# One level of Strassen's algorithm for the second layer's query, key and value projections

## The chip, the cores and the metric

The kernel runs on one core of a Trainium2 chip. The metric is the device time of one execution in microseconds (us). The kernel as it stands takes 2287.54 us (median of three runs, 2286.23 to 2288.77).

## The reference

Two encoder layers run over 1024 tokens of width 1024. Each is a token mixer, a residual sum with layer normalization (LN), a gated feed-forward block (FFN), and again a residual sum with LN. The mixer of the first layer (layer A) is latent attention; that of the second (layer B) is differential attention. What the change touches is the first matrix product of layer B:

```
h = x @ w_in                                  # x (1024, 1024), w_in (1024, 3072)
q, k, v = jnp.split(h, [qk_w, 2 * qk_w], axis=-1)
q = q.reshape(b, s, 8, 2, 64)                 # 8 heads, two softmax maps of width 64
k = k.reshape(b, s, 8, 2, 64)
v = v.reshape(b, s, 8, 128)
...
logits = (q_b . k) * scale - slopes * dist    # per map; a chunk mask on top
a = softmax(map 0) - lam * softmax(map 1)
o = a @ v                                     # then RMS norm per head, and w_o
```

## The kernel before

**Precision.** Every product of float32 values is made of three passes through TensorE. An operand is split into a high part (ScalarE casts it to fp32r) and a low part (VectorE or GpSimd subtracts the high part from the value); the passes are high times high, high times low, low times high (`mm3`, L140 to L145, and L545 or L814 for the FFN). A "split" below is this pair of instructions; `op_unit` (L504) splits one 128x512 block.

**Stages.** The program runs layer A's attention (to about 370 us), its output projection, FFN 0 with its up and down products (to 1079 us), layer B's attention with its projections (1079 to 1495 us and a tail), its output projection, and FFN 1. Both FFNs already use one level of Strassen's algorithm; the projections of layer B don't.

**Around the change.** FFN 0's down product ends with a sum over 11 blocks into four PSUM banks (`dw`, L814), which completes token rows 0 to 3 (a row is a block of 128 tokens); rows 4 to 7 were normalized earlier. `to_xT` (L187) transposes the normalized rows by TensorE and splits them into `xT`, the token operand of the projections, which stays in SBUF in high and low parts. `values_b` (L1262) makes the values of two heads for one row: 24 matmuls with 256 moving columns. `proj_b` (L1281) makes a head's queries or keys for half of the tokens: 24 matmuls with 512 columns; it splits the result straight from PSUM into the layout of the scores (two maps of 64 partitions each; a DMA on GpSimd's queue copies the high part of a query to the other 64 partitions). Weights come by `load_w` (L128), 512 KB each: ScalarE casts 128x1024, GpSimd subtracts 128x1024.

**Order.** A framework's scheduler lays out each engine's instruction order when the program is built; engines then run in that order and wait for each other by semaphores. `attention` (L261) walks through 64 blocks (8 heads with 8 rows of queries). Block `b` issues the scores of block `b + 2`, the transposes of its own softmax, and what `fill` holds for slot `b`. For layer B `fill` puts head 0's projections and values in front of slot 0 and those of head `h` into the slots of head `h - 1`:

```
for j, slot in enumerate((2, 3, 5, 6) if h < H - 1 else (1, 2, 3, 5)):
    at(b + slot, proj_b, h, j // 2, j % 2 if h < H - 1 else 1 - j % 2)
```

At slot 54 `begin_out` (L1410) closes the space of `xT`, and the output projection's weights are loaded there (L361). Nearly all loads and stores are issued by SP, whose queue is in order: a transfer that waits holds up all behind it.

Of the kernel before, what the change touches and what calls it, by code (L numbers as in the profile page):

```python
# [9 lines left out]
F32 = mybir.dt.float32  # L10
# [6 lines left out]
P = 128  # L17
S = 1024
# [20 lines left out]
LAST_ORDER = (6, 7, 4, 5, 2, 3, 0, 1)  # L39


@with_exitstack
def trunk(
# [10 lines left out]
    w_b_qk,  # L54
    w_b_v,
# [131 lines left out]
    def to_xT(y, xT, tb, name, where):  # L187
        hf, c = tb // 4, (tb % 4) * P
        for kq in range(0, KD, 4):
            pt = where[kq // 4](f"xTp_{name}_{kq}")  # L190
            for k in range(4):
                tr(pt[:, k * P:(k + 1) * P], y[:, (kq + k) * P:(kq + k + 1) * P])
            pv = pt.rearrange("p (k t) -> p k t", k=4)
            hi = xT[0][hf][:, kq:kq + 4, c:c + P]
            lo = xT[1][hf][:, kq:kq + 4, c:c + P]
            A.copy(hi, pv)
            V.tensor_tensor(lo, pv, f32(hi), ALU.subtract)

    def new_xT(pool, name):
        t = {  # L200
            (p, hf): pool.tile([P, KD, 512], F32R, tag=f"xT{p}{hf}", name=f"xT{p}{hf}_{name}")
            for hf in range(2) for p in range(2)
        }
        return [[t[p, hf] for hf in range(2)] for p in range(2)]


# [74 lines left out]
    def out_proj(side, w_o, o_dram, x_src, x_dst, lng, lnb, xo):  # L281


        with tc.tile_pool(name="op0", bufs=2, side=side, reuse_waits="tile") as pool:
# [21 lines left out]
            for tb in LAST_ORDER:  # L306
# [152 lines left out]
    def raw_x(y, xo, tb, name):  # L459
# [16 lines left out]
        if tb < 4:  # L476
# [5 lines left out]
            V.tensor_tensor(b21, b21, b12, ALU.add)  # L482
# [33 lines left out]
    def ffn(side, xo, xst, pending, layer, x_src, x_dst, lng, lnb, next_x, spare=()):  # L516
# [211 lines left out]
        pool = st.enter_context(tc.tile_pool(name=f"fd{layer}", bufs=1, side=side, reuse_waits="tile"))  # L728
        stx = ExitStack()
# [182 lines left out]
        else:  # L912
# [11 lines left out]
            junk = wp.tile([P, 2, 512], F32, tag="wr", name=f"junk_{nm}", bufs=2)  # L924
# [6 lines left out]
            for t in range(4):  # L931
# [5 lines left out]
                rest.append(lambda t=t, y=y: to_xT(y, new, t, f"{nm}_{t}", (ps_t, ps_s)))  # L937
# [5 lines left out]
    xs_dr = [dr.tile([S, D], F32, name=f"xs_dr{l}") for l in range(3)]  # L943

# [141 lines left out]
    with ast as st:  # L1086
# [88 lines left out]
        def mix_a(h, g):  # L1175
# [3 lines left out]
            A.copy(ob, po[:, :256])  # L1179
# [15 lines left out]
        for h in range(1, H):  # L1195
# [9 lines left out]
            at(b + (7 if h < H - 1 else 5), k_nope, h, 1)  # L1205
        at(12, constants)
# [12 lines left out]
    xst, wts = ExitStack(), {}  # L1219

    def next_x():
        pool = xst.enter_context(tc.tile_pool(name="xp0", bufs=1, side="right", reuse_waits="tile"))
        wts["v", 0] = [load_w(w_b_v[0, kh], 1024, f"wbv0_{kh}") for kh in range(2)]
        return new_xT(pool, "f0")

    xo, stacks = x_pools("m0", "right")
# [9 lines left out]
    xT, rest, normed = ffn(  # L1236
# [6 lines left out]
    with ExitStack() as st:  # L1243
        lp = st.enter_context(tc.tile_pool(name="b1l", bufs=5, reuse_waits="tile"))
        pool = st.enter_context(tc.tile_pool(name="b1", bufs=2, reuse_waits="tile"))
        ptp = st.enter_context(tc.tile_pool(name="b1p", bufs=4, reuse_waits="tile"))
# [3 lines left out]
        qt = [big_tile(f"bq{j}") for j in range(2)]  # L1250
        kt = [big_tile(f"bk{j}") for j in range(2)]
        ob = big_tile("bo", F32)
        q_hi = [qt[0][:, 0], qt[0][:, 1], qt[1][:, 0]]
# [264 lines left out]
```

## Time and profile before

| what | value |
|---|---|
| median of the runs | 2287.54 us |
| span of the profiled execution (from the page; it gives no other time of that execution) | 2284.9 us |
| TensorE (PE) busy | 2244.2 us, 98% of the span |
| VectorE (DVE), ScalarE (ACT), GpSimd (POOL) busy | 68%, 45%, 38% |
| moved by DMA | 288.28 MB, 126 GB/s on average |
| layer B's projections and most of its attention | 1075 to 1495 us of the span |

"Busy" of PE counts overlapping matmuls once; a matmul of 512 columns is listed with about 390 ns, but the next one starts after about 227 ns. So its cost in a chain of matmuls is read from starts, not from durations. PEld is the loading of weights into the array, which overlaps. A line of a group reads: source line, engine, operation, output and inputs with their shapes, count, busy time, mean of one, and the idle time before. In the list of waits, the figures are total us, times and the longest.

### The profile page before, as it was taken

The numbers are of one execution on the slowest core, as the hardware profiler recorded it, in microseconds if no ns is written. First come the engines' busy times: TensorE is split into PE (matmuls) and PEld (weight loads), VectorE is DVE, ScalarE is ACT, GpSimd is POOL, SyncE is SP. The second block draws the span as 40 slices with busy tenths as digits, with TensorE's granted clock in tenths as the row PEclk, the third lists the DMA queues.
The fourth block names the chain that finished last, engine by engine and source line by source line (L and its number), as shares of the span: only waits on it lengthen the run. The fifth ranks groups of instructions, "written<-read, shape, count | busy, mean of one in ns | idle before, by whom it ended". The sixth has DMA issues, their size and how long they took to land.

```text
span 2284.9 us, 31183 instructions
## 1 busy us (share of the span) xinstructions
PE 2244.2 (98%) x11410; PEld 1910.8 (84%) x11410; DVE 1561.1 (68%) x2901; ACT 1017.7 (45%) x2097; POOL 861.2 (38%) x687
## 2 busy tenths in 40 slices
PE   8999999999999999999999999999999999999997
PEld 8899998878888887888888898987778888887886
DVE  5667675687666658777476766676777666658777
ACT  4455574442333324345465655564432233324353
POOL 2223241114444435455432423221014444436564
PEclk9999999999999999999999999999999999999999
DMA  5010125344344428454311202154254132337353
GB/s 202 14 37 29 41 72 201 138 137 154 144 157 173 157 103 333 176 182 145 106 43 33 70 24 70 29 203 150 92 172 155 70 133 75 134 120 307 140 206 122
DMA packets 105546, 288.28 MB, mean 126 GB/s; under 512 B 7969, under 2 KB 30113, under 8 KB 94897
## 3 DMA queue, kind: packets, MB, share of 16 engines
q1 hardware_dynamic: 100976, 275.87, 34.0%
q0 software_dynamic: 4416, 10.42, 1.6%
q8 instruction: 90, 1.47, 0.3%
q14 instruction: 64, 0.52, 0.1%
HBM read 205.00 MB, written 77.07 MB: 123 GB/s over the span
## 4 chain that ended last, share of the span: by engine, by line
PE 87%; DVE 5%; DMA 3%; ACT 2%; issue 1%; POOL 1%; SPq 0%; DVEq 0%; POOLq 0%; ACTq 0%
PE gb L545 14%; PE gc L545 10%; PE ga L545 8%; PE dw L814 7%; PE s_a L219 4%; PE zp_a L413 4%; PE dx L814 3%; PE s_b L219 3%; PE dv L814 3%; PE dy L814 3%; PE bp L143 3%; PE bp L144 3%; PE bp L145 3%; PE o_a L258 2%; PE o_b L258 2%; PE hq L1019 1%
## 5 line engine op out<-in xcount | busy, mean ns | idle before, releaser
L499 ACT CAST op_g<-gr 128x512 fp32r<-128x512 f32 x240 | 146.8, 621 | 370.8 <-PE gb L545 183.5
L500 POOL TENSOR_TENSOR op_g<-gr,op_g 128x512 fp32r<-128x512 f32 x104 | 145.8, 1407 | 247.6 <-ACT op_g L499 139.4
L500 DVE TENSOR_TENSOR op_h<-rh,op_h 128x512 fp32r<-128x512 f32 x154 | 164.5, 1096 | 62.3 <-ACT op_h L499 62.3
L545 PE MATMUL ga<-xh_m,op_g 128*128 128x512 f32 x512 | 168.1, 389 | 0.0
L499 ACT CAST op_h<-rh 128x512 fp32r<-128x512 f32 x154 | 92.9, 619 | 140.3 <-PE dx L814 37.6
L814 PE MATMUL dw<-op_w_t,op_h 128*128 128x512 f32 x660 | 151.4, 390 | 0.0
L814 PEld LDWEIGHTS dw<-op_w_t,op_h 128*128 128x128 f32 x660 | 123.5, 188 | 26.1 <-DVE op_h L500 0.6
L225 ACT ACTIVATE l_b<-l_b,mx_b 128x256 f32<-128x256 f32 (+7 forms) x128 | 99.5, 778 | 79.2 <-DVE mx_b L222 77.4
L1322 POOL TENSOR_SCALAR l_b<-l_b,r_b,cst 128x128 f32<-128x128 f32 (+3 forms) x64 | 52.8, 825 | 204.1 <-DVE r_b L227 193.2
L814 PE MATMUL dx<-op_w_b,op_h 128*128 128x512 f32 x528 | 123.5, 394 | 5.1 <-ACT op_w_b L499 3.9
L500 POOL TENSOR_TENSOR op_w_t<-tt,op_w_t 128x512 fp32r<-128x512 f32 x66 | 98.1, 1490 | 80.3 <-ACT op_w_t L499 80.3
L814 PEld LDWEIGHTS dx<-op_w_b,op_h 128*128 128x128 f32 x528 | 99.7, 190 | 28.6 <-ACT op_w_b L499 4.7
L500 DVE TENSOR_TENSOR op_g<-gr,op_g 128x512 fp32r<-128x512 f32 x136 | 110.7, 817 | 15.7 <-ACT op_g L499 15.4
L545 PE MATMUL gb<-t4h_f,op_g 128*128 128x512 f32 x352 | 115.9, 390 | 3.4 <-DVE tmp L628 3.4
L500 POOL TENSOR_TENSOR op_g<-s,op_g 128x512 fp32r<-128x512 f32 x40 | 55.2, 1379 | 168.7 <-ACT op_g L499 160.4
L545 PE MATMUL gc<-b22h_f,op_g 128*128 128x512 f32 x352 | 115.4, 389 | 0.8 <-ACT op_g L499 0.8
L545 PE MATMUL gb<-t2h_f,op_g 128*128 128x512 f32 x352 | 115.5, 390 | 0.4 <-DVE op_g L500 0.4
L545 PE MATMUL gc<-t1h_f,op_g 128*128 128x512 f32 x352 | 115.6, 390 | 0.2 <-ACT op_g L499 0.2
L545 PE MATMUL gb<-t3h_f,op_g 128*128 128x512 f32 x352 | 115.2, 389 | 0.0
L545 PEld LDWEIGHTS ga<-xh_m,op_g 128*128 128x128 f32 x512 | 96.1, 188 | 19.9
L143 PE MATMUL bp<-xT_f,h_wb 128*128 128x512 f32 x256 | 103.0, 402 | 0.0
L145 PE MATMUL bp<-xT_f,l_wb 128*128 128x512 f32 x256 | 101.6, 397 | 0.0
(382 smaller groups left out, 6732.8 us busy)
## 6 DMA issues: line engine op xcount, KB each, us to landing
gr<-in_w_gu SPq DMA_DIRECT2D x44, 1024.0 KB, 6.9
rh<-h_dr SPq DMA_DIRECT2D x28, 1024.0 KB, 5.4
h_dr<-sh SPq DMA_DIRECT2D x22, 1024.0 KB, 5.0
h_dr<-hp SPq DMA_DIRECT2D x22, 768.0 KB, 4.1
tt<-in_w_dn SPq DMA_DIRECT2D x22, 512.0 KB, 8.7
rh<-h_dr SPq DMA_DIRECT2D x14, 768.0 KB, 4.4
wo_dr<-op_pwo SPq DMA_DIRECT2D x16, 512.0 KB, 3.3
z<-xs_dr SPq DMA_DIRECT2D x16, 512.0 KB, 10.1
```

What stands on the lines that cost most here:

```text
L143: T.matmul(ps_out, lh, rh, start=(i == 0), stop=False)
L144: T.matmul(ps_out, lh, rl, start=False, stop=False)
L145: T.matmul(ps_out, ll, rh, start=False, stop=(i == n - 1))
L219: T.matmul(s[:, :w], lh, rh[:, ks], start=(j == 0), stop=(j == len(q_pass) - 1))
L225: ends["exp"] = A.activation(l[:, :n], l[:, :n], AF.Exp, bias=mx, scale=-1.0, accum_out=sm).ins
L258: T.matmul(po[:, c], a, b[:, j % 2, c], start=st, stop=sp_, skip_group_check=True)
L413: T.matmul(m, a[:, h, :], self.wo[h][w][:, c], start=(start and h == heads[0] and a is oh and w == 0), stop=(stop and h == heads[-1] and a ...
L499: A.copy(hi, src)
L500: return eng.tensor_tensor(lo, src, f32(hi), ALU.subtract).ins
L545: T.matmul(o, w[:, a, kc], x[b][:, k, :], start=(first and k == 0 and (a, b) == (0, 0)), stop=(k == 3 and a == 1), skip_group_check=True,)
L814: T.matmul(o, h[:, a, c], w[:, b_], start=(first and (a, b_) == (0, 0)), stop=(last and a == 1), skip_group_check=True,)
L1322: G.tensor_scalar(l1[:, :n], l1[:, :n], r1, nlam, ALU.mult, ALU.mult)
```

## The change

The products of `x` with 3072 columns are cut into 12 units of 256 columns: 8 of one head's queries and keys (`qk`), 4 of two heads' values (`v`). In each unit one level of Strassen's algorithm (the form with seven products) halves the inner dimension, the 256 columns and the 1024 tokens. A unit then has products "1" to "7", each of 12 matmuls with 512 columns, and sums around them. The operands change as follows.

- **Weights.** Products 1, 2 and 4 use blocks of the matrix itself (256 KB each, `w_b`); 6, 3, 7 and 5 use sums of blocks. These sums are made during layer A's attention: 48 parts are loaded (`take`), summed in four GpSimd instructions of 128x128 (`combine`) and stored to `ws_dr` (`put`). In layer B each of the 84 operands is loaded and split (ACT, POOL), four products ahead.
- **Tokens.** Rows 4 to 7 are transposed while FFN 0's last down sum still runs (`early`), and are the operands of products 1 and 2. Rows 0 to 3 come by `raw_x`, as in the FFNs. The seven token operands are 2 MB each, in high and low parts. There is room for two of them (`xop`); so all seven are stored to `x_dr`, and the units go through five passes of 3, 3, 3, 2 and 1 units. Pass 0 forms its five operands on the chip, passes 1 to 4 load theirs again from `x_dr` (26 loads of 2 MB). An operand's space is loaded again (`ready`) when its last product has been issued.
- **Results.** The joins of the products are DVE instructions on 128x512. Queries and keys are split, stored to `qk_dr` and fetched from there in the layout of the scores (`fetch_qk`). Values come out transposed and are turned by TensorE (`turned`), 64 transposes in all.
- **Order.** 27 of the 84 products stand in front of the attention, 3 at its start, and 54 in slots 0 to 50.

```diff
@@ out_proj of layer A
+                    elif tb == LAST_ORDER[1]:
+                        behind(i, ends["ob"])
@@ ffn, around FFN 0's last down sum
+        if next_x is not None:
+            next_x.begin()
...
             whole(y4, from_h(2, "4", ("o",)), t4(), False)
+            with tc.high_priority(100):
+                for t in range(4, 8):
+                    next_x.early(z[t], t)
+                for i in range(4):
+                    next_x.weights(i)
             stx.close()
-            new = next_x()
-            with tc.high_priority(60):
-                for t in range(4, 8):
-                    to_xT(z[t], new, t, f"{nm}_{t}", (ps_s, ps_s))
+            new, junk = next_x.open()
...
-                rest.append(lambda t=t, y=y: to_xT(y, new, t, f"{nm}_{t}", (ps_t, ps_s)))
+                rest.append(lambda t=t, y=y: raw_x(y, new, t, f"{nm}_{t}", G))
@@ layer A's attention
+        def combine(i):
+            t = raw_t[i]
+            tc.keep_in_program_order(G.tensor_tensor(t[:, 3], t[:, 2], t[:, 3], ALU.add))
+            G.tensor_tensor(t[:, 2], t[:, 0], t[:, 2], ALU.subtract)
+            G.tensor_tensor(t[:, 0], t[:, 3], t[:, 0], ALU.subtract)
+            G.tensor_tensor(t[:, 1], t[:, 1], t[:, 0], ALU.subtract)
+        for i in range(len(parts)):
+            slot = 6 + i * 7 // 8
+            at(slot, take, i)
+            at(slot + 1, combine, i)
+            at(slot + 2, put, i)
@@ layer B
+        def multiply(u, p, x):
+            w = next_x.ops.pop((u, p))
...
+            for k in range(4):
+                kc = slice(k * P, (k + 1) * P)
+                for a, b in ((0, 0), (0, 1), (1, 0)):
+                    T.matmul(m, w[:, a, kc], x(k, b), start=(p in "1654" and k == 0 and a == b),
+                             stop=(k == 3 and a == 1), skip_group_check=True)
+            while pend:
+                pend.pop(0)()
...
+            elif p == "6":
+                upper[u] = stage("u2", f"u2_{u}")
+                V.tensor_tensor(upper[u], low[u], m, ALU.add)
+            elif p == "7":
+                V.tensor_tensor(low[u], low[u], m, ALU.add)
...
+        def form(x, p):
+            for k in range(4):
+                if p == "6":
+                    t = ws.tile([P, 512], F32, tag="tt", name=f"t2_{k}", bufs=1)
+                    G.tensor_tensor(t, xr["r", 1, 1][:, k], xr["r", 0, 1][:, k], ALU.subtract)
+                else:
+                    t = xr["r", *{"7": (0, 0), "4": (1, 0), "5": (0, 1), "3": (1, 1)}[p]][:, k]
+                split((x[:, k, 0], x[:, k, 1]), t, V)
+                nc.sync.dma_start(x_dr[p][:, k], f32(x[:, k]))
+        def ready(i):
+            if i >= len(operands):
+                return
+            x, p = xop[i % 2], operands[i]
+            if i < 5:
+                form(x, p)
+                return
+            for k in (slice(0, 2), slice(2, 4)):
+                nc.sync.dma_start(f32(x[:, k]), x_dr[p][:, k])
...
-        at(-1, first_values)
-        at(-1, rest[0])
-        at(-1, proj_b, 0, 0, 1)
...
+        advance(4)
+        for t in range(4):
+            rest[t]()
+            if t < 3:
+                advance(2)
+            store(4)
+        ready(0)
+        advance(2)
+        ready(1)
...
+        at(-1, advance, PER)
...
+        for s0, s1, n in (
+            (0, 8, 6), (8, 10, 6), (10, 24, 15), (24, 26, 6), (26, 40, 10), (40, 42, 4), (42, 51, 7),
+        ):
+            for i in range(s1 - s0):
+                at(s0 + i, advance, (i + 1) * n // (s1 - s0) - i * n // (s1 - s0))
```

Three places show how the instructions now stand. The first is PE at the end of FFN 0's last down sum (`dw`). Before, the values of layer B (`bv`) follow, after transposes of rows 6 and 7 (`xTp_f`) that stand ahead of the sum's last matmuls:

```order
L148 MATMUL xTp_f_6_0_10082<-ident,z_6_8620 128x128 x4
L148 MATMUL xTp_f_6_4_10089<-ident,z_6_8620 128x128 x4
L148 MATMUL xTp_f_7_0_10096<-ident,z_7_8621 128x128 x4
L148 MATMUL xTp_f_7_4_10103<-ident,z_7_8621 128x128 x4
L814 MATMUL dw_2_9093<-op_w_t_10_10018,op_h_4_10_10014 128x512 x2
L814 MATMUL dw_3_9094<-op_w_t_10_10018,op_h_4_10_10014 128x512 x2
L143 MATMUL bv_4_10202<-h_wbv_0_10040,xT_f_10052 128x256
```

The same place now: the transposes of rows 4 to 7 (`xTe`) stand further up, among the sum's matmuls, and product 1 of the first unit (`bp_1`) follows the sum directly.

```order
L803 MATMUL dw_0_9484<-op_w_t_10_10411,op_h_4_10_10407 128x512 x2
L803 MATMUL dw_1_9485<-op_w_t_10_10411,op_h_4_10_10407 128x512 x2
L803 MATMUL dw_2_9486<-op_w_t_10_10411,op_h_4_10_10407 128x512 x2
L803 MATMUL dw_3_9487<-op_w_t_10_10411,op_h_4_10_10407 128x512 x2
L1412 MATMUL bp_1_10617<-x1h_10426,op_b_1_10500 128x512
L1412 MATMUL bp_1_10617<-x1lh,op_b_1_10500 128x512
```

The second is PE at the start of pass 0, where product 2 of the sixth unit ends (`x2h`, `x2l` are the early token operand) and product 6 begins, the first that needs rows 0 to 3 (`xop`). Before there was no such place.

```order
L1412 MATMUL bp_1_10862<-x2l,op_b_2_10838 128x512
L1412 MATMUL bp_1_10862<-x2h,op_b_2_10838 128x512
L1412 MATMUL bp_6_10986<-xop_10523,op_b_6_10859 128x512
L1412 MATMUL bp_6_11006<-xop_10523,op_b_6_10923 128x512
L153 MATMUL vT_0_10957<-ident,ct_00_10938 128x128 x4
L1412 MATMUL bp_6_10986<-xop_10523,op_b_6_10859 128x512 x2
L1412 MATMUL bp_6_11006<-xop_10523,op_b_6_10923 128x512 x2
```

Here the products 6 of two units are interleaved, so that one slice of the token operand feeds both before the next slice is needed.

The third is SP's queue. Before, in the first part of layer B, it held weights (`r_wb`, `r_wbv`) and the stores of the normalized rows:

```order
L132 DMA r_wb_0_10332<-in_w_b_qk 128x1024
L1248 DMA bb<-in_c_bias_b 128x1024
L132 DMA r_wb_1_10558<-in_w_b_qk 128x1024
L184 DMA xs_dr_98<-y_f_0_10110 128x1024 x2
L132 DMA r_wb_0_10774<-in_w_b_qk 128x1024
L184 DMA xs_dr_98<-y_f_1_10111 128x1024 x2
L132 DMA r_wb_1_10994<-in_w_b_qk 128x1024
```

Now, at the change from pass 0 to pass 1, loads of token operands (`xop`), of weights (`rw`), stores of results (`qk_dr`) and the first fetches of queries (`bq`) stand between each other:

```order
L1459 DMA xop_10524<-x_dr_114 128x2048
L1288 DMA rw_6_11253<-ws_dr_103 128x4x128
L1398 DMA qk_dr_10_128<-out_11_11280 128x1024
L1398 DMA qk_dr_00_122<-out_01_11304 128x1024
L1288 DMA rw_6_11286<-ws_dr_104 128x4x128
L1459 DMA xop_10523<-x_dr_115 128x2048
L1288 DMA rw_7_11308<-ws_dr_103 128x4x128
L1468 DMA bq_11360<-qk_dr_00_122 64x2x512
L1459 DMA xop_10523<-x_dr_115 128x2048
L1398 DMA qk_dr_00_126<-out_01_11352 128x1024
```

Over the whole program SP issues 809 transfers in place of 447. What is added: 52 loads of 1024 KB (`xop`), 20 stores of 512 KB and 16 of 256 KB (`x_dr`), 84 loads of 256 KB (`rw`), 32 stores of 512 KB (`qk_dr`), 80 fetches of 256 KB (`bq`, `ql`, `bk`), 6 of 256 KB for partial results, and in layer A 48 loads and 48 stores of 256 KB. What is removed: 24 loads of 512 KB, and GpSimd's 32 copies of 128 KB.

More of the change, by code (lines that the diff above doesn't have):

```diff
@@ L1281, in proj_b, with chain_bank @@
-        def proj_b(h, which, hf):
-            if (which, h) not in wts:
-                wts[which, h] = load_w(w_b_qk[h, which], 1024, f"wb{h}_{which}")
-            wh, wl = wts[which, h]
+        ql_t = [pool.tile([P, S], F32R, tag=f"ql{j}", name=f"ql{j}", bufs=1) for j in range(2)]
+        low, upper, chains, pend = {}, {}, {}, []
+        state = {"s": 4, "out": None, "bank": 0}
+        def chain_bank(name):
+            state["bank"] += 1
+            return (ps_m if state["out"] is None or state["bank"] % 2 else ps_t)(name)
```

337 lines of the change are left out of this document (231 added, 106 removed).

## The prediction

> **What bounds the kernel now.** I read the page's head and its chain of waits, then busy time by stage, then who waits for whom, then single matmuls.
>
> ```profile
> span 2284.9 us, 31183 instructions
> PE 2244.2 (98%) x11410; PEld 1910.8 (84%) x11410; DVE 1561.1 (68%) x2901; ACT 1017.7 (45%) x2097; POOL 861.2 (38%) x687
> ...
> PE 87%; DVE 5%; DMA 3%; ACT 2%; issue 1%; POOL 1%; SPq 0%; DVEq 0%; POOLq 0%; ACTq 0%
> ```
>
> The chain that ended last is PE for 87% of its length, DMA for 3%. By stage (columns: length; busy time of PE, PEld, DVE, ACT, POOL; clock; DMA share; GB/s):
>
> ```profile
> 75.00:370.00 295.00, 294.07 (x1866) 266.51 (x1865) 201.90 (x575) 172.68 (x435) 98.08 (x98) 1.00 0.20 62
> 1075.00:1495.00 420.00, 418.03 (x2576) 373.15 (x2575) 273.93 (x792) 237.65 (x538) 140.54 (x131) 1.00 0.19 56
> 1500.00:1520.00 20.00, 18.14 (x101) 14.96 (x102) 15.50 (x47) 9.87 (x24) 2.33 (x3) 1.00 1.01 418
> ```
>
> The changed stage is the second row: PE is busy for 418 of 420 us, while DVE, ACT and POOL stand at 65%, 57% and 33% and the DMA engines at 19%. The first row is layer A's attention, where the weight sums go. The third is a stretch in which DMA was full; it shows what full means: 418 GB/s. Waits of PE in the stage are few:
>
> ```profile
> PE pt_b L148 <- DVE l_b L1323: 4.3, 3, 1.9
> ...
> PE xTp_f L148 <- DVE y_f L183: 0.8, 1, 0.8
> ```
>
> So matmul time taken out of this stage comes out of the whole, as long as nothing else becomes late.
>
> **What is removed from PE.** The listed durations overlap, so I take starts. A run of twelve FFN matmuls, a run of seven transposes, and a row of values whose starts lie 25 matmuls apart:
>
> ```profile
> 552.30 2.72 PE ga L545 x12
> ...
> 1512.98 0.77 PE pt_b L148 x7
> ```
>
> ```profile
> 1080.99 0.28 PE L144 MATMUL bv<-l_wbv,xT_f 128*128 128x256 f32 x1
> ...
> 1083.98 0.28 PE L145 MATMUL bv<-h_wbv,xT_f 128*128 128x256 f32 x1
> ```
>
> A matmul of 512 columns costs 2.72 / 12 = 0.2267 us, one of 256 columns (1083.98 - 1080.99) / 25 = 0.1196 us, a transpose 0.11 us. The two kinds stand in three lines of 256 each, of which these are the first:
>
> ```profile
> L143 PE MATMUL bp<-xT_f,h_wb 128*128 128x512 f32 x256 | 103.0, 402 | 0.0
> ...
> L143 PE MATMUL bv<-h_wbv,xT_f 128*128 128x256 f32 x256 | 73.1, 286 | 0.0
> ```
>
> Before: 768 x 0.2267 + 768 x 0.1196 = 174.1 + 91.9 = 266.0 us. After: 84 products of 12 are 1008 x 0.2267 = 228.5 us, and 64 turns of values 64 x 0.11 = 7.0 us. The transposes of the tokens are as many as before. **PE saves 30.5 us.** That is 11%, not the 12.5% that seven products in place of eight suggest, since the turns are new.
>
> **What is added elsewhere.** Durations of like instructions:
>
> ```profile
> L499 ACT CAST op_g<-gr 128x512 fp32r<-128x512 f32 x240 | 146.8, 621 | 370.8 <-PE gb L545 183.5 <-PE gc L545 90.0 <-DVE gr L578 38.5
> L500 POOL TENSOR_TENSOR op_g<-gr,op_g 128x512 fp32r<-128x512 f32 x104 | 145.8, 1407 | 247.6 <-ACT op_g L499 139.4 <-DVE tmp L636 105.3 <-DMA pwo<-in_w_o_b 2.6
> L137 POOL TENSOR_TENSOR l_wb<-r_wb,h_wb 128x1024 fp32r<-128x1024 f32 x16 | 38.4, 2404 | 49.4 <-ACT h_wb L136 39.7 <-issue 8.4 <-ACT pth_b L246 1.3
> L636 DVE TENSOR_TENSOR tmp<-tmp,gc 128x512 f32<-128x512 f32 x40 | 27.5, 686 | 26.7 <-PE gc L545 26.7
> L1308 DVE TENSOR_TENSOR bk<-bp,bk 64x512 fp32r<-64x512 f32 x32 | 22.0, 689 | 7.1 <-ACT bk L1307 6.3
> L1277 DVE TENSOR_TENSOR bvl<-bv,bvh 128x256 fp32r<-128x256 f32 x32 | 13.4, 420 | 11.8 <-ACT bvh L1276 11.7
> ```
>
> DVE: 60 joins, 32 low parts of queries and values and 24 token instructions at 0.69 us, 20 low parts of token operands at some 0.9 make 98 us; 64 low parts of queries and keys at 0.69, 32 of values at 0.42 and 16 of tokens go, 68 us. It stands then at (274 + 30) / 390 = 78%. ACT gains some 28 us, to 68%. POOL: 84 weight splits and 32 others at 1.41 us make 163 us; 16 weights at 2.40, 8 more at some 2.6 and 32 DMA issues go, 77 us; (141 + 86) / 390 = 58%. None is full. In front of the attention POOL is near it: 23 weights and 16 sums of tokens are 55 us in some 73 us.
>
> DMA is another matter. The list in the section on the change adds 124.5 times 1024 KB in layer B (52 + 14 + 21 + 16 + 20 + 1.5), or 130.5 MB; now 420 us x 56 GB/s = 23.5 MB are moved there, of which 16.8 go. After: 137 MB. At 418 GB/s they fill 328 us of a stage of 390 us: **the DMA share rises from 19% to about 84%**, and small pieces cost more. Times from issue to landing (KB each, us):
>
> ```profile
> gr<-in_w_gu SPq DMA_DIRECT2D x44, 1024.0 KB, 6.9
> ...
> wo_dr<-op_pwo SPq DMA_DIRECT2D x16, 512.0 KB, 3.3
> ...
> of_a<-o_dr SPq DMA_DIRECT2D x8, 512.0 KB, 4.6
> zy_a<-in_x SPq DMA_DIRECT2D x8, 512.0 KB, 3.5
> ...
> pwo<-in_w_o_b SPq DMA_DIRECT2D x16, 256.0 KB, 4.0
> ```
>
> `of_a` comes in pieces of 512 B, like the weight sums from `ws_dr`, and lands 1.1 us later than `zy_a` of the same size. A token operand is two loads of 1024 KB, 5.0 us of full DMA, and lands after 7 to 9 us.
>
> **The terms that give time back**, each with its bounds:
>
> - *Start of pass 0 (second order excerpt).* After the last transposes of row 3 PE has 22 matmuls, 5.0 us. Meanwhile one slice of product 6's operand needs a copy (0.6), a POOL subtraction behind one POOL instruction that may be running (1.4 to 2.8), a cast (0.6) and a subtraction (0.7): 3.3 to 4.7 us and the handing over. The queue behind it on PE is all of pass 0. 0 to 4 us; I take **2**, the near end, since the chain just fits.
> - *From pass 0 to pass 1 (third excerpt).* In pass 0 PE works 15 x 2.72 + 2 = 43 us. DMA has 20 stores of operands (25 us at 418 GB/s), 18 weights of 256 KB (0.6 to 1.2 each, some 16 us), 6 stores of results (7.5), 6 partial results (4) and the load of the next 6 (5): 50 to 57 us. By the difference, 7 to 14 us, the load of 6 would be late; some of the stores may still run when it does, and the next 7 and the first queries stand behind it in the same queue. 0 to 15; I take **6**.
> - *Other operand loads.* In the attention two products with their attention work take about 10 us, a load 7 to 9; where slots hold three products (8 to 10, 24 to 26) two products take 8. 8 such places at 0 to 1 us: 0 to 8, I take **3**.
> - *The last pass.* One unit, so a new operand for each 2.72 us of matmuls: seven in nine slots, some 5.8 us each, against 5.0 of token load and 1.5 to 2.5 of others. 0 to 12, with two loaded ahead; I take **3**.
> - *Layer A.* 192 GpSimd instructions of 128x128. Near rows: a POOL scaling of 128x128 takes at least 438 ns, a quarter of a split 352 ns. 192 x 0.44 = 84 us put POOL at (98 + 84) / 295 = 62%, and the softmax scaling queues behind up to 1.8 us of them, with two blocks of slack ahead of the transposes. 0 to 10; I take **2**.
>
> ```profile
> L1322 POOL TENSOR_SCALAR l_b<-l_b,r_b,cst x64: 438/824/1212, 1136.4 to 1547.2; 128x128 f32<-128x128 f32 x8, 128x256 f32<-128x256 f32 x8, 128x384 f32<-128x384 f32 x8, 128x512 f32<-128x512 f32 x8
> ```
>
> - *Longer softmax chains in layer B* from fuller DVE, ACT and POOL. A DVE split with both inputs in SBUF takes 0.69 us when POOL rests and 1096 ns on the mean of the down products where POOL works:
>
> ```profile
> 1071.79 0.69 DVE L500 TENSOR_TENSOR op_h<-rh,op_h 128x512 fp32r<-128x512 f32 x1 [2.03 <-ACT op_h L499]
> ```
>
> ```profile
> L500 DVE TENSOR_TENSOR op_h<-rh,op_h 128x512 fp32r<-128x512 f32 x154 | 164.5, 1096 | 62.3 <-ACT op_h L499 62.3
> ```
>
> The softmax join (L1323) is of this kind, 0.4 us more for each of 54 blocks at the worst 22 us; two blocks of lookahead cover most. 0 to 16; I take **2**.
> - *The tail.* The weights of the output projection wait for the last projection today, and are on the chain for 10 us:
>
> ```profile
> 1496.49 10.06 DMA wo<-wo_dr
> ```
>
> The last product now stands three slots earlier. -4 to 0; I take **-1**.
>
> Sum: -30.5 + 2 + 6 + 3 + 3 + 2 + 2 - 1 = **-13.5 us**. The profiled span of 2284.9 us becomes 2271.4; the median of the runs lies 2.6 us above that span, so I forecast **2274 us**.
>
> **Rivals.**
>
> *All is hidden.* For it: 84% is not 100%, a load of an operand takes less than the 12.6 us that an average operand has (390 / 31), and DMA is 3% of the chain today. Then 2287.5 - 30.5 = **2257 us**. Against it: the count of pass 0, where DMA has more to do than PE.
>
> *DMA becomes the bound (slower).* Place: the 26 loads of token operands, which PE meets in its fixed order, so that a late operand also holds up the attention behind it. Each is late by the backlog ahead of it in SP's order. The terms that are no operand loads give back 2 + 2 + 2 - 1 = 5 us; with (30.5 - 5) / 26 = 1.0 us of lateness for each load the saving is gone, and from there on it is slower. At 1.5 us: -30.5 + 5 + 39 = +13.5, **2301 us** (the forecast has 12 / 26 = 0.46 us). For it: 137 MB in pieces down to 512 B at a share of 84% or more, and one operand of prefetch. Against: the 12.6 us per operand. In "DMA: Bandwidth & Descriptors", section "Specifications", the Trainium skill gives a limit of about 358 GB/s of HBM for each core. By it 137 MB take 383 us by estimate, nearly the whole stage, and this rival would be the likeliest. The trace differs: the third row above has 418 GB/s, with this core alone at work.
>
> *Contention eats the saving (no change).* The softmax chain grows by 0.3 us for each of 54 blocks past its cover, 16 us in place of 2: -13.5 + 14 = 0, **2288 us**. For it: DVE at 78%, POOL almost doubled. Against: PE waits 4.3 us for that chain today.
>
> **How the numbers follow.** Forecast 46%, all hidden 15%, no change 18%, slower 21%. About 0.2% (4.6 us) is what a measurement of this kernel tells from no change. Faster is the forecast and the first rival, 0.61; same 0.18; slower 0.21. The forecast's own range is 2262 to 2282. For 8 in 10 it goes from 2253 (all terms at their near ends: -30.5 - 4) to 2297, short of the slow rival.
>
> **What would show it.** In the profile after: 1008 `bp` matmuls with starts 0.227 us apart; a DMA share of 0.8 or more in the stage, near 1 around the change of pass; PE waits for `xop<-x_dr`, 6 us at that change and a few more in the last pass; PE busy of layer A's window within 2 us in length. If waits for `xop` sum to over 30 us, the slow rival holds; if the stage is 30 us shorter, the first; if waits of `pt_b` for `l_b` grow past 15 us, the third. I am wrong altogether if the time is lost outside layer B's stage.

## The result

The changed kernel takes **2355.16 us** (median of four runs, 2349.25 to 2355.94); the kernel before took 2288.15 us beside it (2286.23 to 2289.6). The ratio is 1.0287, with a 95% interval from 1.0275 to 1.0299: **67 us slower**, where 2274 us, 13.5 us faster, had been predicted. 2355 us lies outside the range of 2253 to 2297 us. It is also past the slow rival's 2301 us. The trace of the changed kernel is that of its fastest run (2349.25 us), so a difference between two traces can come out some 6 us other than the one between the medians.

### The profile page after: what moved, and what is told of

Its sections match the earlier page's. It is cut to its first block, busy times and chain, and to the rows that moved or that the text cites. A ratio compares the mean times of both kernels' runs of the same rounds, so it can differ in the third digit from the quotient of the medians.

```text
span 2347.4 us, 31278 instructions
## 1 busy us (share of the span) xinstructions
PE 2251.4 (96%) x10946; PEld 1882.1 (80%) x10946; DVE 1597.0 (68%) x2925; ACT 1032.7 (44%) x2145; POOL 1024.7 (44%) x936
## 4 chain that ended last, share of the span: by engine, by line
PE 33%; DMA 8%; DVE 5%; issue 2%; ACT 1%; SPq 1%; POOL 1%; DVEq 0%; POOLq 0%; ACTq 0%
PE gb L532 7%; PE gc L532 5%; PE ga L532 5%; PE zp_a L400 3%; PE bp L1412 3%; DMA rw<-ws_dr 2%; PE dw L803 2%; PE dx L803 1%; PE s_b L204 1%; PE dv L803 1%; PE dy L803 1%; DMA rw<-in_w_b 1%; PE o_b L243 1%; PE pt_b L153 1%; DVE op_h L487 1%
## 5 line engine op out<-in xcount | busy, mean ns | idle before, releaser
L1412 PE MATMUL bp<-xop,op_b 128*128 128x512 f32 x864 | 235.2, 412 | 26.8 <-ACT op_b L486 10.5
L1412 PEld LDWEIGHTS bp<-xop,op_b 128*128 128x128 f32 x864 | 163.3, 196 | 70.6 <-ACT op_b L486 14.1
L487 DVE TENSOR_TENSOR op_h<-rh,op_h 128x512 fp32r<-128x512 f32 x154 | 161.9, 1079 | 62.5 <-ACT op_h L486 62.4
L487 POOL TENSOR_TENSOR op_b<-rw,op_b 128x512 fp32r<-128x512 f32 x84 | 114.2, 1361 | 125.4 <-ACT op_b L486 120.0
L487 POOL TENSOR_TENSOR op_g<-s,op_g 128x512 fp32r<-128x512 f32 x40 | 54.5, 1362 | 168.1 <-ACT op_g L486 159.9
```

Source lines behind the costliest of these rows:

```text
L487: return eng.tensor_tensor(lo, src, f32(hi), ALU.subtract).ins
L1412: T.matmul(m, w[:, a, kc], x(k, b), start=(p in "1654" and k == 0 and a == b), stop=(k == 3 and a == 1), skip_group_check=True)
```

## Time and profile after

The head of the changed kernel's page, and the shares of the chain that ended last (it could be followed back only to 1171 us, so its shares sum to about half of the span):

```profile
span 2347.4 us, 31278 instructions
PE 2251.4 (96%) x10946; PEld 1882.1 (80%) x10946; DVE 1597.0 (68%) x2925; ACT 1032.7 (44%) x2145; POOL 1024.7 (44%) x936
...
PE 33%; DMA 8%; DVE 5%; issue 2%; ACT 1%; SPq 1%; POOL 1%; DVEq 0%; POOLq 0%; ACTq 0%
```

PE has 464 matmuls fewer and is still busy 7 us longer. The span grew by 62.5 us. Marks in the two traces say where (start of the instruction named, us):

| mark | before | after | later by |
|---|---|---|---|
| first matmul of layer A's output projection (`zp_a`) | 346.8 | 358.0 | 11.2 |
| first up product of FFN 0 (`ga`) | 440.2 | 453.6 | 13.4 |
| first projection of layer B | 1080.9 | 1096.8 | 15.9 |
| first score of layer B (`s_b`) | 1130.2 | 1219.2 | 89.0 |
| last projection | 1495.0 | 1534.9 | 39.9 |
| last `o_b` of layer B's attention | 1559 | 1617 | 58 |
| end | 2284.9 | 2347.4 | 62.5 |

So some 16 us are lost ahead of layer B, 42 in it, and 4.5 behind its attention. Busy time by stage in the kernel before (columns as in the prediction: length; busy time of PE, PEld, DVE, ACT, POOL; clock; DMA share; GB/s). The rows are the projections ahead of the first score, and the attention with the projections in its slots:

```profile
1081.00:1130.00 49.00, 48.18 (x320) 44.19 (x319) 25.38 (x46) 19.91 (x42) 20.86 (x18) 1.00 0.35 108
1130.00:1562.00 432.00, 425.53 (x2565) 375.45 (x2564) 295.06 (x877) 252.38 (x582) 136.48 (x131) 1.00 0.22 72
```

The same stretches of the changed kernel:

```profile
1097.00:1219.00 122.00, 100.76 (x416) 76.65 (x414) 61.65 (x85) 49.13 (x92) 65.72 (x50) 0.92 0.89 307
1219.00:1620.00 401.00, 372.62 (x1994) 308.12 (x1995) 297.39 (x858) 238.47 (x574) 161.97 (x149) 0.98 0.87 282
```

Two losses are read from such a row: PE idle is length less PE busy, and the clock's part is the length times what the clock lacks of 1. Ahead of the first score that is 21 + 10 us (before: 1 + 0), in the attention 28 + 8 us (before: 6 + 0). Together 67 us against 7. The balance (+62.5 against -30.5 + 16 + 60) leaves some 17 us that these columns don't show; by the starts of the matmuls (a table at the end of the experiments) some 15 of it lie in layer B, in gaps so short that a row counts them as busy. The DMA share is 0.89 and 0.87, as predicted.

Waits of PE in the first of these stretches of the changed kernel (total us, times, longest):

```profile
PE bp L1412 <- ACT op_b L486: 8.2, 5, 2.8
PE bp L1412 <- POOL op_b L487: 2.8, 4, 0.9
PE vT L153 <- DVE u L1436: 2.5, 1, 2.5
PE bp L1412 <- ACT xop L486: 2.1, 1, 2.1
PE bp L1412 <- DVE xop L487: 1.9, 1, 1.9
PE bp L1412 <- DMA xop<-x_dr: 1.4, 1, 1.4
```

The products wait 11 us for the split of their weights (`op_b`) and 1.4 us for a token operand's load. And the only wait of PE at layer A's output projection, with what ACT waited for there:

```profile
PE zp_a L148 <- ACT ob L1175: 8.0, 1, 8.0
...
ACT ob L1175 <- DMA o_dr<-ob: 6.6, 1, 6.6
```

The first `zp_a` waits for ACT's copy of the last attention output `ob`, which waits until an earlier `ob` has been stored. The kernel before has no wait at this place, though its last `ob` is copied as late (354.1 us; in the changed kernel 357.5).

## Experiments

Times are medians; the kernel before took 2287.8 to 2289.4 us beside them. First places, then causes.

**e1: the added edge in layer A's output projection.**

```diff
-                    elif tb == LAST_ORDER[1]:
-                        behind(i, ends["ob"])
```

> The changed kernel without one edit: in the first layer's output projection the split of the second row of oh_a no longer stands behind the last copy of ob. Theory A (the edit puts the first matmul zp_a behind a copy that itself waits for a store of ob to land): zp_a starts within 2 us of the last o_a again, PE has no half-clock stretch there, and about 11 us go: 2344 us. Theory B (the last copy of ob frees the bank that zp_a needs, whatever the order of the splits): zp_a still starts 8 us late, 2355 us.

Measured: 2355.28 us; the wait of `zp_a` for `ob` is 8.0 us again. The edge isn't the cause. What is left is the PSUM bank: after the attention the kernel opens a new set of PSUM tiles on the same banks, and the first `zp_a` must wait for the copy of `ob` if it gets the bank of the last `o_a`. The traces don't record the banks, nor why the framework places tiles as it does; e5 and e11 test it from outside.

**e5: another bank for the last o_a.**

```diff
-        po = ps_o(f"o_{name}")
+        po = (ps_t if name == "a7_0" else ps_o)(f"o_{name}")
```

> The changed kernel with the last o_a of the first layer in a bank of the transposes' three (in place of one of the three of the m tiles). Theory A (the planner put the last o_a into the bank that the first zp_a uses, which it had not before the change): zp_a starts right after the last o_a, at about 350 in place of 358, without a half-clock stretch, and 9 to 11 us go: 2344 to 2346 us. Theory B (zp_a waits for ACT's place in order): it starts at 358 again, 2355 us.

Measured: 2348.56 us (2339.73 to 2351.26), 7 us less. The stretch in which the changed kernel's PE stood still, in e5:

```profile
350.00:358.00 8.00, 8.00 (x37) 6.62 (x36) 1.27 (x2) 1.64 (x4) 0.00 (x0) 1.00 0.97 344
```

PE works through it at full clock, and layer B's projections start at 1086 in place of 1097. The last copy of `ob` still waits 6.4 us for its store; `zp_a` no longer waits for it. Theory A holds for the place. Of these 10 us, some 3 don't reach the end; the runs of this kernel lie 12 us apart, and where the rest went isn't settled.

**e11: the weight sums of layer A left out** (beside e4, below).

```diff
-        for i in range(len(parts)):
-            slot = 6 + i * 7 // 8
-            at(slot, take, i)
-            at(slot + 1, combine, i)
-            at(slot + 2, put, i)
```

> The kernel of e4 with the weight sums left out of the first layer's attention as well (48 loads, 192 GpSimd operations, 48 stores; products 6, 3, 7 and 5 have wrong weights as there). Theory A (the sums cost the first layer 3 us in its attention, and by their place in the planner's simulated time they also moved the last o_a into the bank of zp_a): the last o_a at 347, zp_a right behind it, projections start 14 to 16 us earlier than in the changed kernel, 2337 to 2342 us. Theory B (the sums are hidden; the wait in the output projection comes from elsewhere): 2350 us or more.

Measured: 2349.37 us, 4 us less than e4 and between the two theories. The place is as theory A has it: the last `o_a` ends 1.5 us earlier than in e4, `zp_a` follows it at 348 without a wait, and the projections start at 1083.5, 12 us earlier than in e4 (1095.5). So the sums cost 1.5 us in layer A's attention, near the 2 of the prediction, and another 10 by bringing about the wait of `zp_a`; that they do so by way of the bank is argued from e5, not shown. As in e5, part of the front's gain is missing at the end, here 8 of 12 us; that stays open.

**e2: token operands not loaded again.**

```diff
-            for k in (slice(0, 2), slice(2, 4)):
-                nc.sync.dma_start(f32(x[:, k]), x_dr[p][:, k])
+            return
```

> The changed kernel with the 26 loads of token operands in passes 2 to 5 left out (52 DMAs of 1024 KB, 54.5 MB); the products there use what stands in xop from the first pass, so their values are wrong; all else runs. Theory A (full DMA engines bound the second layer's projection stage): first score s_b 25 to 30 us earlier, PE waits of bp for op_b and xop below 5 us in the stage, 2310 to 2320 us. Theory B (products wait for their weights, two raw buffers in one ordered queue; the amount of data is secondary): the first pass and the change to the second stay slow, 2335 to 2345 us.

Measured: 2338.01 us, 17 us less, and the first score only 7 us earlier. With 54.5 MB less to move, most of the loss is still there at the end, as theory B has it. The DMA share falls from 0.87 to 0.53 in the attention, but stays at 0.82 ahead of the first score, so that e2 alone doesn't rule out full DMA engines there; e6 does.

**e4: all weights from one source.**

```diff
-  src = ws_dr[u][:, :, {"6": 0, "3": 1, "7": 2, "5": 3}[p]].rearrange("k p c -> p k c")
+  src = w_b[u, :, {"6": 0, "3": 1, "7": 2, "5": 3}[p]].rearrange("p (k c) -> p k c", k=4)
```

> The changed kernel with all product weights loaded from w_b, 2 KB in a piece; the sums in ws_dr (512 B in a piece) are made and stored as before but not read, so products 6, 3, 7 and 5 have wrong weights. Theory A (pieces of 512 B make weights late): rw lands in 3 us in place of 3 to 8, 10 to 20 us go, 2335 to 2345 us. Theory B (not the pieces, but what stands ahead of them in the queue or on the engines): within 5 us, 2350 to 2360 us.

Measured: 2353.35 us. The pieces of 512 B cost nothing that these runs can tell (2 us, within the spread); the weights land in 4.7 us at the median, no sooner than in the changed kernel (4.3).

**e3: weights by GpSimd's queue.**

```diff
-                nc.sync.dma_start(raw, src)
+                nc.gpsimd.dma_start(raw, src)
```

> The changed kernel with the loads of product weights (rw) issued by GpSimd in place of SyncE: they no longer queue behind operand loads and stores that wait for something, and those no longer behind a weight load that waits for GpSimd's split. Same bytes. Theory A (full DMA engines): within 5 us of the changed kernel, 2350 to 2360 us. Theory B (order in SyncE's queue): 15 to 25 us go between the start of the projections and the first score, 2330 to 2340 us.

Measured: 2377.85 us, 23 us *more*: both theories miss. The weights come no sooner by their own queue (one in 5.0 us, 4.7 us to land), but each issue now takes GpSimd's time, in the order of its splits, so whether SP's order costs anything by itself stays open (issues of the weights ahead of the first score in e3; duration ns min/median/max):

```profile
L1288 POOL DMA_DIRECT2D rw<-ws_dr x17: 747/764/781, 1141.2 to 1236.3; - x17
```

**e6: four weights on their way in place of two.**

```diff
-            while self.n[0] < min(len(stream), i + RAWS):
+            while self.n[0] < min(len(stream), i + (RAWS if self.more is None else RAWS + MORE)):
...
-                raw = self.raw[u, p] = self.pool.tile([P, 4, P], F32, tag="rw", name=f"rw{u}_{p}")
+                where = self.pool if self.more is None or self.n[0] % (RAWS + MORE) < RAWS else self.more
+                raw = self.raw[u, p] = where.tile(
+                    [P, 4, P], F32, tag="rw", name=f"rw{u}_{p}", bufs=RAWS if where is self.pool else MORE)
```

`MORE` is 2, and `more` is the staging pool of layer B.

> The changed kernel with four buffers for product weights on their way from DRAM in place of two (the other two out of the pool of the second layer's staging, so except around the change of that pool). Theory A (two in flight at 4.9 us to landing plus 2 us of split limit a product to one in 4 us): between the first product from xop and the first score PE waits for op_b fall from 11 to below 4 us, 10 to 18 us go, 2337 to 2345 us. Theory B (the DMA engines are full; more in flight only lengthens each): within 5 us, 2350 to 2360 us.

Measured: 2330.44 us, 25 us less (ratio to before 1.019, interval 1.0174 to 1.0205). Casts of weights from 1130 to 1222 us, in the changed kernel and in e6 (count; ns min/median/max; first and last start):

```profile
L486 ACT CAST op_b<-rw x20: 613/620/622, 1129.8 to 1216.9; 128x512 fp32r<-128x512 f32 x20
```

And in e6:

```profile
L487 ACT CAST op_b<-rw x24: 615/619/625, 1132.2 to 1211.9; 128x512 fp32r<-128x512 f32 x24
```

One weight came in (1216.9 - 1129.8) / 19 = 4.6 us before, in (1211.9 - 1132.2) / 23 = 3.5 us now, and PE takes 2.72 us for a product. Loads didn't get faster; from issue to landing of the weights ahead of the first score, changed kernel and e6:

```profile
DMA to landing us min/median/max: 2.6/4.3/8.9
```

And in e6:

```profile
DMA to landing us min/median/max: 2.8/5.5/10.9
```

Theory A holds, and more than its 10 to 18 us go: with two buffers, the time on the way set the pace. The engines had room, since the DMA share ahead of the first score rises from 0.89 to 0.92 with the faster pace. PE's wait for `op_b` is gone from e6's list for the stretch, and the next thing stands at its head:

```profile
PE bp L1417 <- DMA xop<-x_dr: 6.8, 2, 3.7
```

**e9: e5 and e6 together.**

> The changed kernel with both edits of e5 and e6: another bank for the first layer's last o_a, and four buffers for product weights on their way. Theory A (two causes in two places, independent): 7 + 25 = 32 us go, 2321 to 2327 us. Theory B (they share their gain, or the planner moves other work): 2330 us or more.

Measured: 2326.05 us (ratio 1.0157, interval 1.014 to 1.0174): 29 us less, within theory A's range: the two gains add up, as far as the spread lets one say. It is the best version of the change with right values here, and still 37 us slower than the kernel before.

**e7: most weights not loaded.**

```diff
-                nc.sync.dma_start(raw, src)
+                if self.n[0] < 12:
+                    nc.sync.dma_start(raw, src)
+                    self.kept = raw
+                else:
+                    self.raw[u, p] = self.kept
```

> The changed kernel with the last 72 of 84 weight loads left out (18.9 MB); those products split again what the twelfth weight brought, so their values are wrong, the splits stay. Theory A (weights on their way set the pace of passes 1 and 2): first score 20 to 30 us earlier, 2320 to 2333 us. Theory B (token operands are the late ones): at most 8 us, above 2347 us.

Measured: 2323.83 us, 31 us less, as theory A has it. At the end, 18.9 MB of weights cost nearly twice what 54.5 MB of token operands cost. The first score comes 11 us earlier, not 20 to 30: part of the gain lies in the attention, where weights were late too.

**e8: neither weights nor operands loaded** (the edits of e7 and e2).

> The changed kernel with both left out: the 26 loads of token operands and the last 72 weight loads (73 MB of 130), values wrong. Theory A (DMA, by time on its way or by volume, is what ate the saving in the second layer): with out-projection A's 11 us still in it, 2290 to 2305 us. Theory B (the longer chains of DVE, ACT and GpSimd and the missing fill at the end of the attention): above 2320 us, with waits of pt_b, s_b and ms unchanged.

Measured: 2307.68 us, 31 + 17 = 48 us less, between the theories. DMA lateness cost 48 us at the end. But with these loads gone, with 30 us less matmul time, the kernel is still 20 us slower than before. Its two stretches:

```profile
1096.00:1198.00 102.00, 93.72 (x424) 75.56 (x423) 64.12 (x85) 51.48 (x96) 74.27 (x54) 0.97 0.75 273
1198.00:1582.00 384.00, 367.91 (x1995) 310.36 (x1996) 293.61 (x858) 236.21 (x569) 159.57 (x145) 0.97 0.42 128
```

16 us of idle time and 12 us of clock are lost in the attention, where the kernel before loses 6. Either the added work of the other engines does that or the missing matmuls.

**e13: the splits of these weights left out too** (in the edit `self.same` is the split of the twelfth weight).

```diff
-                self.ops[u, p] = op_unit(self.raw.pop((u, p)).rearrange("p k c -> p (k c)"), G, f"b{u}_{p}")
+                raw = self.raw.pop((u, p))
+                if i < 12:
+                    self.same = op_unit(raw.rearrange("p k c -> p (k c)"), G, f"b{u}_{p}")
+                self.ops[u, p] = self.same
```

> The kernel of e8 with the splits of the last 72 weights left out as well (72 casts of ScalarE at 0.62 us, 72 subtractions of GpSimd at 1.29 us); those products use the split of the twelfth weight, values wrong. Theory A (what is left of the loss in the attention is contention for ScalarE and GpSimd): PE's loss from the first score to the last o_b falls by 10 us or more from 55, 2285 to 2297 us. Theory B (it is missing fill: fewer matmuls, and more of them ahead of the attention): that loss stays within 6 us, 2299 to 2307 us, and what goes is ahead of the first score.

The loss of 55 us in this text is measured another way: each start of a matmul less the one before, over the usual spacing of its kind. With the median spacings of the kernel before, the two traces give 42 us for e8 and 45 for e13; the 55 must rest on other spacings. Measured: 2308.15 us, the same as e8, and a us past theory B's range; the loss hasn't fallen, and nothing went ahead of the first score either. The attention's row:

```profile
1197.00:1583.00 386.00, 370.81 (x1992) 312.21 (x1993) 284.49 (x857) 212.53 (x521) 95.56 (x97) 0.96 0.41 126
```

POOL works 64 us less and ACT 24 us less than in e8, and PE gains nothing. Contention with the splits is not it. e8's trace shows what is, beside the same part of the kernel before (both from the last projection to the last `o_b`):

```profile
1452.00:1579.00 127.00, 111.24 (x588) 89.78 (x587) 101.10 (x301) 76.41 (x188) 32.33 (x35) 0.92 0.49 162
```

And before:

```profile
1495.00:1559.00 64.00, 58.68 (x329) 49.16 (x328) 48.40 (x136) 36.34 (x89) 16.81 (x18) 1.00 0.53 204
```

In e8, 127 us of the attention run after the last projection in place of 64, and nearly all of e8's idle time in the attention (15.8 of 16.1 us) and most of its half clock lies there. But for three splits of values, the splits and joins of the change are over by then.

**e10: the kernel before with an eighth of the projections' matmuls left out.** Nothing is added anywhere; this is the saving alone.

```diff
-                for k in range(KD)
+                for k in range(KD - 1)
```

> The kernel before, with one of eight contraction slices left out of the second layer's query, key and value projections (values wrong): 96 matmuls of 512 columns and 96 of 256 less, 96 x 0.2267 + 96 x 0.1196 = 33.2 us of PE time, nothing added anywhere. Theory A (the attention's own chains are hidden, so matmul time taken out comes out of the whole, as the prediction assumed): 30 to 33 us go, 2255 to 2258 us. Theory B (these matmuls also fill the time in which the softmax chains run; with less fill PE waits there): 10 to 22 us go, 2266 to 2278 us.

Measured: 2278.57 us (2277.14 to 2279.97), ratio 0.9957, interval 0.9945 to 0.997: of 33.2 us taken out, **10.7 us reach the end** (7 to 13): theory B, at its edge (these are medians; the traces differ by 8.5 us). Its attention, and what PE waits for in it:

```profile
1126.00:1552.00 426.00, 408.61 (x2406) 356.32 (x2405) 302.16 (x877) 251.07 (x582) 136.95 (x131) 0.98 0.23 72
```

And PE's waits there (total us, times, longest):

```profile
PE zp_a L413 <- DMA wo<-wo_dr: 4.7, 1, 4.7
PE s_b L219 <- DVE mx_b L222: 4.3, 7, 1.4
PE pt_b L148 <- DVE l_b L1323: 2.8, 4, 1.0
PE pt_b L148 <- DVE nmu_a L166: 1.8, 1, 1.8
PE pt_b L148 <- DVE ptl_b L247: 1.5, 2, 0.7
```

The kernel before has in the same stretch 4.3 us for `l_b` and 1.1 and less for the rest. Now the maxima of the softmax (`mx_b`) and the load of the output projection's weights (`wo`) show: 17 us of idle time and 8 of clock are lost in the attention, nearly as much as in e8 (16 + 12). These matmuls had been the cover of those chains. Not all of it is softmax: some 10 us are lost in one place (1481.5 to 1497), most of them by the wait for `wo`, whose load is issued at 1478.9, after the last projection, and lands 12.1 us later, and by the half clock around it.

**e12: work for PE while it waits.** In the changed kernel, between the last `o_a` and the first `zp_a`:

```diff
+        if name == "a7_0":
+            fill = ps_s("fill")
+            for i in range(64):
+                t = T.matmul(fill[:, :256], vh, hi[:, 0, 0:256], start=True, stop=True)
+                behind(t.ins, end)
```

> The changed kernel with 64 matmuls of 256 columns (64 x 0.118 = 7.6 us) into an unused bank between the last o_a of the first layer and the first zp_a, which waits 8 us there anyway; their result is used nowhere. Theory A (TensorE's clock is halved after it has stood still for some 2 us, so each such wait costs a second time): no half-clock stretch at 353 to 363, zp_a starts at 358 as before, projections start about 5 us earlier, 2348 to 2351 us. Theory B (the half clock there has another cause): the stretch stays, 2355 to 2357 us.

Measured: 2352.43 us (2349.3 to 2356.13), too near the changed kernel's spread to tell by the time. The wait and the 5 us behind it, changed kernel and e12:

```profile
349.00:358.00 9.00, 1.04 (x11) 0.90 (x9) 2.68 (x4) 2.43 (x6) 0.07 (x1) 0.70 0.99 349
358.00:363.00 5.00, 5.00 (x12) 3.94 (x13) 1.22 (x1) 1.90 (x3) 3.03 (x2) 0.52 0.87 284
```

And in e12:

```profile
349.00:358.00 9.00, 9.00 (x73) 8.74 (x73) 2.52 (x3) 2.84 (x5) 0.00 (x0) 1.00 0.97 358
358.00:363.00 5.00, 5.00 (x24) 4.13 (x23) 1.22 (x1) 1.35 (x3) 2.54 (x2) 1.00 0.88 262
```

`zp_a` starts at nearly the same time, but 24 matmuls fit where 12 did: with PE kept busy the clock isn't halved. Theory A holds for the clock; it is worth 2.4 us here, not 5, since half of the 10 us at half clock lay in the wait itself.

**Where layer B loses its time, by the starts of the matmuls.** For each matmul I take its start less the one before, less the median spacing of its kind in the kernel before (0.227 us for 512 columns, 0.120 for 256, 0.109 for 128, and so on). The sums are us of PE time lost:

| run | ahead of the first score | from there to the last projection | from there to the last `o_b` | length of this last part |
|---|---|---|---|---|
| before | 1.0 | 8.2 | 9.1 | 64 |
| changed kernel | 34.3 | 38.9 | 19.8 | 82 |
| e2, no operand loads | 27.5 | 15.7 | 42.5 | 131 |
| e7, most weights not loaded | 18.1 | 21.4 | 29.9 | 106 |
| e8, neither | 12.4 | 5.5 | 36.5 | 127 |
| e10, kernel before with fewer matmuls | 1.8 | 22.4 | 17.2 | 72 |

Up to the last projection the changed kernel loses 73.2 us and e8 17.9: late loads cost 55 us there. Without them the projections are through earlier, more of the attention is left with nothing in between, and 17 us are lost again. e2 gains 30 us up to the last projection (73.2 - 43.2) and e7 34 (73.2 - 39.5): up to there the operand loads cost nearly as much as the weights, with three times the bytes, but e2 loses more of it behind.

## Why the prediction was wrong

Two steps failed: the prediction let the whole saving reach the end, and it priced the new loads by their bytes. The second is the larger: late loads cost 55 us up to the last projection (table above), where the terms for them add up to 12 (6 + 3 + 3).

**The first is the value of the saving.** "So matmul time taken out of this stage comes out of the whole, as long as nothing else becomes late": the 30.5 us were counted right (the products are spaced as assumed) and entered the sum in full. The row that seemed to show it, PE busy 418 of 420 us with 4.3 us of waits, shows a stage whose chains are *covered*, not one without chains. (The 4.3 us are also those of the whole program; within 1075 to 1495 us the wait for `l_b` is 1.1 us, and most of it comes after the last projection, where the cover ends.) e10 measures the term: about a third reaches the end. In the change there is less cover still: 364 matmuls of 512 columns, 82 us, run ahead of the first score in place of 45 us (96 of 512 and 192 of 256 columns), so the attention has 146 us of projections above it where it had 221. What that costs shows where no projection is left: 20 us are lost there in the changed kernel (9 before), and 37 in e8, where the projections end sooner. The prediction had a term for longer softmax chains (+2) but none for the same chains with less above them.

**The start of layer B and the change of pass: the loss is there, its size and cause are not as priced** (+2 and +6; 31 us of idle time and clock before the first score against 1). The prediction summed bytes: 18 weights at 0.6 to 1.2 us each. It named the load of product 6's operand as the one to be late. What was late is the weights, 256 KB each: 4.3 us to land at the median, 0.62 on ACT and 1.29 on GpSimd until the buffer is free, so 6.2 us for each of two buffers, 3.1 us for a product at the best and 4.6 as measured, where PE takes 2.72. e6 shows that by two buffers more, e7 by no loads. What makes 4.6 of 3.1 stays open; a weight that can't be issued yet because of others ahead of it in SP's queue would be one way. The operands' loads come second here (e2: 7 us ahead of the first score).

**Other operand loads and the last pass** (+3 and +3): PE waits 6.8 us for `xop<-x_dr` in all of the changed kernel, about as said. Without these loads 17 us go at the end (e2), and 30 up to the last projection, of which 23 behind the first score. PE's waits by name are only a part of what they cost. How the rest comes about isn't settled; it isn't half clock, of which e2 has more (68 us against 55).

**Layer A** (+2): its attention is 3 us longer, and e11 gives 1.5 for the sums. The wait for the bank was not seen: 8 us of waiting and 2.4 of half clock (e5, e12). Some 3 us more in FFN 0 have no experiment. In its last sentence the prediction said it would be wrong altogether if time were lost outside layer B; 16 of 62 us were.

**Tail** (-1): PE no longer waits for the weights of the output projection (their loads are issued from 1540 us, its first matmul starts at 1570), but nothing covers the last blocks. In the changed kernel 82 us pass from the last projection (1535) to the last `o_b` (1617); before, 64 us.

**The rivals.** The slow one had the right sign and a part of the mechanism: token operands late at each of 26 loads. Up to the last projection these loads do cost 30 us, 1.2 for each, near its 1.0 to 1.5; it didn't see the weights, the end of the attention or layer A. Its limit from the Trainium skill ("DMA: Bandwidth & Descriptors", section "Specifications", about 358 GB/s of HBM for a core) would make the bytes the bound. The trace doesn't agree: stretches of the changed kernel move 402 to 428 GB/s (rows of the last section), and 54.5 MB (e2) are worth no more than 18.9 MB (e7). The "no change" rival, contention of the other engines, falls with e13, and with e8, which loses only 6 us from the first score to the last projection with all splits and joins at work. That all is hidden falls with the result.

The sum of what the runs showed, for the profiled execution: -30.5 for matmuls, +16 ahead of layer B, +33 ahead of the first score, +31 from there to the last projection, +11 from there to the last `o_b`, read from the table of starts, and some 3 behind it; that is +63, where 62.5 were measured.

## What to carry to other kernels

A stage with PE at 99% may be balanced rather than PE-bound: take some of its matmuls out, as e10 does, before building anything that saves matmuls there, and price the saving by what then shows. Price a stream of small operands by buffers over time on the way (landing, splits, release), not by bytes: two buffers of 256 KB at 6 us each could not feed a product of 2.72 us. Look at what is left without cover: in e2 and e8 a part of the time gained ahead of the last projection was lost again behind it. After any change look at the places that it doesn't touch; here one cost 8 us of waiting.

## What the runs showed of the hardware

A wait of PE of some 2 us can cost a second time. In three examples of the changed kernel PE is busy for 1.3 to 1.7 of 3.4 us, and in the following 3.4 us, or a multiple, the clock is half (rows: the stretch ahead and the one behind; the busy time of the second holds matmuls of double length):

```profile
1134.20:1137.60 3.40, 1.26 (x7) 0.73 (x5) 2.16 (x2) 3.33 (x7) 2.63 (x2) 1.00 0.94 327
1137.60:1147.80 10.20, 8.35 (x20) 5.84 (x21) 6.74 (x8) 3.79 (x7) 6.25 (x6) 0.50 1.04 402
1321.90:1325.30 3.40, 1.72 (x8) 0.77 (x7) 3.09 (x11) 2.36 (x9) 2.11 (x3) 1.00 1.03 325
1325.30:1328.70 3.40, 3.40 (x10) 2.68 (x11) 3.05 (x12) 1.59 (x6) 1.16 (x2) 0.51 1.02 304
1557.50:1560.90 3.40, 1.43 (x6) 0.59 (x4) 2.48 (x8) 2.17 (x6) 1.19 (x1) 1.00 1.02 428
1560.90:1564.30 3.40, 2.96 (x12) 2.44 (x11) 2.59 (x8) 2.01 (x5) 0.00 (x0) 0.50 1.00 417
```

Not every such wait does: cut into stretches of 3.4 us, as the half clock begins and ends, the changed kernel has eight at full clock with PE busy for under 1.5 us, and half clock follows each; it has ten with 1.5 to 1.9 us, and half clock follows three of them.

Between 100 and 2260 us the kernel before has one such stretch (3.4 us), the changed kernel eleven (55 us), e10 four (24 us); half of that is lost at most, up to 27 us in the changed kernel. The Trainium skill ("TensorE: Matmul & The Clock Gate", section "Part 1: The HAM clock gate (the "warmup" mystery)") has windows of 3.4 us after which the clock falls to half, and calls them idle windows. The length agrees. But here the window need not be idle: a third to a half of busy time in it did not keep the clock.
